# Norm parts at the seam between mixer 1 and block 1b moved; row minima of both mixers chained through a start value, masks added on VectorE

## The chip, the cores and the metric

The kernel runs on one core of a Trainium2 chip. The core has TensorE (PE; its weight loads are shown as PEld), VectorE (DVE), ScalarE (ACT), GpSimd (POOL) and the queue of SyncE (SP), which issues most DMAs. The metric is the device time of one execution in microseconds; lower is better.

## The reference

The model has two layers over 512 latent tokens and 256 context tokens, with 1024 channels. Each layer is a half SwiGLU block, an attention mixer and another half SwiGLU block; each of the three is modulated before and closed by a layer norm:

```python
def ffn_sublayer(h, shift, scale, gate, w_in, w_out, g, b):
    y = swiglu(modulate(h, shift, scale), w_in, w_out)
    return layer_norm(ALPHA * h + FFN_RES * gate * y, g, b)
```

Mixer 0 is neighbourhood attention: each query sees a window of 256 keys with a learned bias, and all 256 context keys. Mixer 1, the one at the centre of this case, works in blocks of 128 queries:

```python
valid = ((jnp.abs(pos_q[:, None] - pos_k[None, :]) <= WA_WINDOW)
         & (pos_k >= 0)[None, :] & (pos_k < S)[None, :])
s_win = jnp.where(valid, jnp.einsum('bqhgd,bkhd->bhgqk', qb, kb).astype(jnp.float32), NEG_INF)
s_ctx = jnp.einsum('bqhgd,bkhd->bhgqk', qb, kc).astype(jnp.float32)
s_sink = jnp.broadcast_to(sink, s_win.shape[:-1] + (1,))
p = jax.nn.softmax(jnp.concatenate([s_win, s_ctx, s_sink], axis=-1), axis=-1)
```

So a row of scores has up to 384 window keys, 256 context keys and one sink logit, and its maximum goes over all three. In layer 1 the context tokens need no output, so what follows mixer 1 handles the 512 latent tokens alone. The output is the latent stream after layer 1.

## The kernel before

**Layout.** Activations lie with channels on the 128 partitions and tokens along the row: eight tiles `z` for the stream. A matmul operand is split into a rounded part and a rest (`uh`, `ul` for activations, `wh`, `wl` for weights), and a full product is three matmuls (`mm3`, L160 to L167). Weights come by DMA on SP's queue into `wr`; ACT makes `wh` (L103) and POOL or DVE makes `wl` (L105).

**Order.** The stages are 0a, mixer 0, 0b, 1a, mixer 1, 1b. The program is written in an order of its own, and a scheduler that simulates the engines sets the final order of each engine's queue when the kernel is built. Two means steer it. `plan` (L147) hangs functions on named points, and `at` (L151) runs them when the program comes by, for example `wo7_3` (after the last attention block of head pair 7) or `pd1b_0_0_4` (after the fifth down product of 1b's first chunk). `behind` (L343) orders two instructions of one engine. `keep_back` holds an instruction behind which each following accumulation (`accumulate`, L499 to L502: z plus gate times product, on DVE) is ordered; `back` sets it.

**A layer norm** (`layer_norm`, L432, and `ln`) is a list of parts: sums over the eight `z` tiles (DVE and POOL, L352), the mean by a matmul with a matrix of 1/1024 (`pm`, L447), centring (L369) with squares on ACT (L456) and their sum, the variance by matmuls (`pv`, L472) with a reciprocal root by tiny DVE operations (`rstd`, L477 and L359 to L364), a spread of the root over the partitions by matmuls (`pr`, L400), then for each channel tile the normalisation (L485), the modulated `uf` (L319), `uh` (L321) and `ul` (L326), and last `kept`, which scales `z` for the residual (L340, POOL). In the lists `l4[0]` (tokens 0 to 255, after mixer 1) and `l4[1]` (tokens 256 to 511) the indices 0 to 6 are sums, mean, centring, variance, spread, normalisation with modulation, kept.

**The seam.** Mixer 1 handles the last two head pairs (6 and 7) in two halves of the tokens: attention for tokens 0 to 255, their output products (`pow`, `w3_0`), attention for tokens 256 to 511, their output products (`w3_1`, banks `c` and `s` in turn, four in all). Each half has eight output products of six matmuls. Block 1b then opens with tokens 0 to 255: two pairs of products `pa1b`, `pv1b` (24 matmuls each), eight down products `pd1b` (on the two banks of `s`), then the same for tokens 256 to 511. The first needs `l4[0]`, the second `l4[1]`.

**Attention of mixer 1** (`attn`, L1193). Each of 8 head pairs has four blocks, and each block two heads: 64 heads in all. The scores (negated, so that the row maximum is a minimum) go into a bank `s` by two matmuls for the window (L1213, L1214) and two for the context (L874, L875). The band mask is added by PE: an identity times a 128 x 128 mask in bf16, for the first and for the last 128 columns of the window (L1216, L1218), 96 such matmuls in all. Edge blocks (0 and 3) have 256 window columns beside 256 of the context in one bank, middle blocks (1 and 2) have 384, and their context scores go to a bank `c`. DVE takes the minimum (L1226, in middle blocks also L1222) and combines it with the sink (L1230, in middle blocks L1228). ACT computes the exponentials and their sums (L1238 to L1242), DVE the reciprocal, POOL scales (L917), PE transposes (L898), and PE multiplies by the values (L908).

**Attention of mixer 0** (`lat`, L993) does the like for 64 latent heads: a minimum over the context (L1019), a reduction that adds the bias and takes the minimum over the window (L1020), a tiny operation for the smaller of both (L1022), then the exponential (L1024).

**Buffers.** The tag `v` of phase `S` holds 256 columns a buffer: the value tiles of the mixers and the `uf` tiles of norms over 256 tokens, 9 buffers. `mk` is a working tile into which the mask is loaded; DVE casts it to bf16 (L1118).

Of the kernel before, what the change touches and what calls it, by code (L numbers as in the profile page):

```python
# [8 lines left out]
F32 = mybir.dt.float32  # L9
F32R = mybir.dt.float32r  # L10
BF16 = mybir.dt.bfloat16
I32 = mybir.dt.int32
AF = mybir.ActivationFunctionType
# [5 lines left out]
P = 128  # L19
# [10 lines left out]
BIG = 1e30  # L30
# [8 lines left out]
def hybrid_kernel(ctx: ExitStack, tc: tile.TileContext, h0, cc, crow, wmod, wmodt, bmod, lnp, wst,  # L39
# [13 lines left out]
    def t2(nm, tag="t2"):  # L53
        return tp.tile([P, 512], F32, tag=tag, name=nm, bufs={"t2": 6, "ln": 2, "sl": 2}[tag])
# [245 lines left out]
    def mod_out(nm, d, c0, c1, st, prm, rm=False, dd=None):  # L300
# [204 lines left out]
    def ffn(nm, groups, gt, mid, post, units=(), opened={}, head=None, apart=None):  # L505
# [312 lines left out]

        def back(x):
            keep_back[0] = x  # L820

# [68 lines left out]
    def vtile(nm):  # L890
        return ph["S"].tile([P, 256], F32, tag="v", name=nm, bufs=9)

# [26 lines left out]
    def small(tag, nm):  # L919
        return tp.tile([P, 2], F32, tag=tag, name=nm, bufs=4)  # L920
# [26 lines left out]
    def na_mixer(gt):  # L947
# [45 lines left out]
        def lat(qd, pr, st, oh, ol, cbs=range(4)):  # L993
# [15 lines left out]
            for cb in cbs:  # L1009
                pts = []  # L1010
                qc = slice(cb * P, (cb + 1) * P)
                for h in range(2):
# [7 lines left out]
                    nc.vector.tensor_tensor_reduce(out=ps[:, 0:256], in0=ps[:, 0:256], in1=nbs[h][:, (0, 1, 1, 2)[cb], :],  # L1020
                                                   scale=1.0, scalar=BIG, op0=ALU.add, op1=ALU.min, accum_out=m[:, 1:2])
                    nc.vector.tensor_tensor(out=m[:, 0:1], in0=m[:, 0:1], in1=m[:, 1:2], op=ALU.min)  # L1022
                    p = t2(f"p{nm}")
                    last_exp[0] = nc.scalar.activation(p[:], ps[:], AF.Exp, bias=m[:, 0:1], scale=-1.0, accum_out=l[:, 0:1])  # L1024
                    nc.vector.reciprocal(l[:, 0:1], l[:, 0:1])  # L1025
# [77 lines left out]

    mkb = cp.tile([P, 2, P], BF16, name="mkb")
    idb = cp.tile([P, P], BF16, name="idb")
    nc.vector.tensor_copy(idb[:], idn[:])

    def wa_mixer(gt):
# [3 lines left out]
        for i in range(2):  # L1112
            t = gp.tile([P, NL], F32, tag="gs", name=f"rc{i}", bufs=6)
            nc.sync.dma_start(t[:], ropec[:, i, :])
            rc.append(t)
        mk = t2("mk")
        nc.sync.dma_start(mk[:, 0:256], wmask[:])
        nc.vector.tensor_copy(mkb[:].rearrange("p a b -> p (a b)"), mk[:, 0:256])  # L1118

# [73 lines left out]
        def attn(s, q, oh, ol, bs=range(4), tags=("t", "mm")):  # L1193
# [5 lines left out]
            def sink(h):  # L1199
                return nsink[:, hd + 4 * h:hd + 4 * h + 1]  # L1200

            for b in bs:
# [5 lines left out]
                split = nw + NC > 512  # L1208
                mc, lc = (small("mc", f"mc{nm}"), small("lc", f"lc{nm}")) if split else (None, None)
                pw, pc = [], []  # L1210
                for h in range(2):
                    pb = bank("s", f"sw{nm}_{h}")
                    nc.tensor.matmul(pb[:, 0:nw], q[h][:, qc], k[h][:, k0:k1], start=True, stop=False)  # L1213
                    nc.tensor.matmul(pb[:, 0:nw], q[h][:, qc], k[2 + h][:, k0:k1], start=False, stop=False)  # L1214
                    if b > 0:
                        nc.tensor.matmul(pb[:, 0:P], idb[:], mkb[:, 0, :], start=False, stop=b == 3)  # L1216
                    if b < 3:
                        nc.tensor.matmul(pb[:, nw - P:nw], idb[:], mkb[:, 1, :], start=False, stop=True)  # L1218
                    pb2 = bank("c", f"sc{nm}_{h}")[:, 0:NC] if split else pb[:, nw:nw + NC]
                    scores(pb2, q[h], k[h], k[2 + h], qc, slice(NL, NT))  # L1220
                    if split:
                        nc.vector.tensor_reduce(out=mc[:, h:h + 1], in_=pb2, axis=AX.X, op=ALU.min)  # L1222
                        pc.append(pb2)
                        pb = pb[:, 0:nw]
                    mh = m[:, h:h + 1]
                    nc.vector.tensor_reduce(out=mh, in_=pb, axis=AX.X, op=ALU.min)  # L1226
                    if split:
                        x = nc.vector.scalar_tensor_tensor(out=mh, in0=mh, scalar=mc[:, h:h + 1], in1=sink(h), op0=ALU.min, op1=ALU.min)  # L1228
                    else:
                        x = nc.vector.tensor_tensor(out=mh, in0=mh, in1=sink(h), op=ALU.min)  # L1230
                    pw.append(pb)
# [168 lines left out]
    def whole(x, head):  # L1400
# [22 lines left out]
    plan(wa_4=l3[1][1:3], wa_7=l3[1][3:4], wq0_0=l3[1][4:6], wq0_1=l3[0][6:] + l3[1][6:])  # L1423
    plan(wo6_2=l4[0][:1], wo6_3=l4[0][1:2], wm7_3=l4[0][2:3], wo7_3=l4[0][3:4], pow3_1_256_2=l4[0][4:6],
         pow3_1_256_7=l4[1][:1])
    wa_mixer(gate(1, 5, 1.0))
    plan(pa1b_0_0_0=l4[0][6:], pv1b_0_0_0=l4[1][1:3], pd1b_0_0_3=l4[1][3:4], pd1b_0_0_7=l4[1][4:])
    ffn("1b", g1, lambda: gate(1, 8, 0.5), None, final, apart=True)
# [126 lines left out]
```

## Time and profile before

| What | Value |
|---|---|
| Median of three runs | 2750.59 us (2749.0 to 2759.77) |
| Profiled execution, own time | 2756.96 us |
| Its span, first to last instruction | 2755.2 us |
| Granted clock of TensorE, mean | 0.986 |
| Busy: PE, DVE, ACT, POOL | 2646.0, 1851.5, 1206.2, 1665.0 us |
| DMA | 311.92 MB, mean 113 GB/s |

Busy times are of one execution; the shares overlap, since the engines run side by side. In the slices of the profile each digit is a fortieth of the span (about 69 us) and gives the busy share in tenths. A PE that is busy is not necessarily at its peak: matmuls overlap in the pipeline, so their durations sum to more than their stretch of time. In a timeline the brackets show how long the engine stood idle before an instruction and what ended that.

### The profile page before, as it was taken

What the parts mean: (1) busy time and instruction counts of PE and PEld (TensorE: products, weight loads), DVE (VectorE), ACT (ScalarE), POOL (GpSimd) and SP (SyncE); (2) the same over time, 40 slices, a digit from 0 to 9 for tenths busy, and PEclk for the clock granted to TensorE, in tenths of its full rate; (3) what the DMA queues carried; (4) which work ended last, traced back from release to release, by engine and by line L of the source; (5) the groups of instructions that cost most, each with busy time, mean ns of one, the idle gap of its engine ahead of it and who ended that gap; (6) DMA issues with size and microseconds to landing.
All of it is one profiled execution on the core that took longest, in us unless ns stands there. A gap on an engine that the chain in (4) does not pass through costs nothing. (4 is left out here: it accounts for less than half of the span.)

```text
span 2755.2 us, 47890 instructions
## 1 busy us (share of the span) xinstructions
PE 2646.0 (96%) x16954; PEld 2415.7 (88%) x16954; DVE 1851.5 (67%) x4238; ACT 1206.2 (44%) x2505; POOL 1665.0 (60%) x1522
## 2 busy tenths in 40 slices
PE   8999999999999989999999999999998999899997
PEld 5799998887888889999998889999987777899997
DVE  4877777775555687656565766666577767677765
ACT  5244343366445344343432534343336655444442
POOL 4786766464433566867664668666645445567762
PEclk9999999999999999999999999999999999999998
DMA  9367565522221213444443225556632111245551
GB/s 330 93 176 200 141 167 148 149 78 66 58 58 49 72 47 93 117 126 128 120 135 106 75 77 146 141 143 179 192 118 64 32 32 45 64 104 127 135 144 56
DMA packets 295615, 311.92 MB, mean 113 GB/s; under 512 B 27856, under 2 KB 193872, under 8 KB 294352
## 3 DMA queue, kind: packets, MB, share of 16 engines
q1 hardware_dynamic: 278960, 279.36, 34.0%
q0 software_dynamic: 16128, 29.37, 6.4%
q8 instruction: 134, 2.20, 0.3%
q14 instruction: 105, 0.86, 0.1%
q10 hardware_dynamic: 288, 0.14, 0.0%
HBM read 300.92 MB, written 12.25 MB: 114 GB/s over the span
## 5 line engine op out<-in xcount | busy, mean ns | idle before, releaser
L105 POOL TENSOR_TENSOR wl<-wr,wh 128x512 fp32r<-128x512 f32 x200 | 261.1, 1322 | 155.9 <-ACT wh L103 78.1
L105 POOL TENSOR_TENSOR wl_s<-S,wh_s 128x512 fp32r<-128x512 f32 x240 | 317.8, 1360 | 45.4 <-ACT wh_s L103 44.9
L103 ACT CAST wh_s<-S 128x512 fp32r<-128x512 f32 x256 | 155.3, 620 | 415.6 <-POOL S L641 128.3
L641 POOL TENSOR_TENSOR S<-wr,wr 128x512 f32<-128x512 f32 x128 | 173.5, 1355 | 202.3 <-DMA wr<-in_wst_dram 188.3
L212 DVE CUSTOM_DVE_ANT_0 jk<-wt,cb 128x512 f32<-128x512 f32 x360 | 244.9, 680 | 22.8 <-DMA wt<-in_wmodt_dram 18.6
L105 POOL TENSOR_TENSOR wl_a<-wr,wh_a 128x512 fp32r<-128x512 f32 x144 | 189.1, 1361 | 15.6 <-ACT wh_a L103 12.7
L103 ACT CAST wh_a<-wr 128x512 fp32r<-128x512 f32 x192 | 118.7, 621 | 153.2 <-PE pd1b L166 20.2
L103 ACT CAST wh<-wr 128x512 fp32r<-128x512 f32 x200 | 121.0, 618 | 91.6 <-DMA wr<-in_wst_dram 17.5
L500 DVE SCALAR_TENSOR_TENSOR z<-pd0b,gt,z 128x256 f32<-128x256 f32 (+1 forms) x168 | 97.0, 595 | 43.0 <-PE pd0b L167 42.3
L500 DVE SCALAR_TENSOR_TENSOR z<-pd1a,gt,z 128x512 f32<-128x512 f32 (+1 forms) x150 | 88.7, 606 | 34.9 <-PE pd1a L167 27.5
L917 POOL TENSOR_SCALAR p<-p,l 128x512 f32<-128x512 f32 x64 | 44.4, 695 | 109.6 <-DVE l L1025 109.1
L500 DVE SCALAR_TENSOR_TENSOR z<-pd0a,gt,z 128x512 f32<-128x512 f32 (+1 forms) x160 | 93.4, 613 | 14.4 <-PE pd0a L167 14.1
L641 POOL TENSOR_TENSOR S<-wr,S 128x512 f32<-128x512 f32 x64 | 90.4, 1413 | 3.5
L641 POOL TENSOR_TENSOR S<-S,wr 128x512 f32<-128x512 f32 x64 | 90.3, 1411 | 3.1
L340 POOL TENSOR_SCALAR z<-z,ag_None,ab_None 128x256 f32<-128x256 f32 (+1 forms) x77 | 57.9, 755 | 51.2 <-DVE uh L325 33.6
L917 POOL TENSOR_SCALAR pw<-pw,l 128x512 f32<-128x512 f32 (+1 forms) x64 | 40.9, 640 | 76.2 <-DVE l L1252 31.6
L1024 ACT ACTIVATE p<-s,m 128x512 f32<-128x512 f32 x64 | 44.0, 688 | 81.5 <-DVE m L1022 76.7
L326 DVE TENSOR_TENSOR ul<-ufl,uh 128x256 fp32r<-128x256 f32 (+1 forms) x88 | 59.7, 685 | 6.9 <-ACT uh L321 5.4
L319 ACT ACTIVATE ufl<-z,bi_None,sc_None 128x256 f32<-128x256 f32 (+1 forms) x77 | 48.2, 638 | 26.1 <-DVE z L485 25.7
L500 DVE SCALAR_TENSOR_TENSOR z<-pd1b,gt,z 128x512 f32<-128x512 f32 (+1 forms) x91 | 53.3, 619 | 9.2 <-PE pd1b L167 6.6
L164 PE MATMUL vn<-wh,uh 128*128 128x256 f32 x192 | 54.9, 286 | 0.9 <-DVE nq L861 0.5
L166 PE MATMUL vn<-wl,uh 128*128 128x256 f32 x192 | 54.4, 283 | 0.0
(1488 smaller groups left out, 10636.2 us busy)
## 6 DMA issues: line engine op xcount, KB each, us to landing
wr<-in_wst_dram SPq DMA_DIRECT2D x456, 256.0 KB
wt<-in_wmodt_dram SPq DMA_DIRECT2D x206, 256.0 KB
wr_0b<-in_wst_dram SPq DMA_DIRECT2D x47, 256.0 KB
wr_1b<-in_wst_dram SPq DMA_DIRECT2D x47, 256.0 KB
wr_2b<-in_wst_dram SPq DMA_DIRECT2D x47, 256.0 KB
wr_3b<-in_wst_dram SPq DMA_DIRECT2D x47, 256.0 KB
wm<-in_wmod_dram SPq DMA_DIRECT2D x8, 1024.0 KB
zspare<-in_wmodt_dram SPq DMA_DIRECT2D x30, 256.0 KB
```

Of the source, the lines that this page charges most:

```text
L103: nc.scalar.copy(hi[:], src[:])
L105: x = eng.tensor_tensor(out=lo[:], in0=src[:], in1=hi[:].bitcast(F32), op=ALU.subtract)
L164: behind(nc.tensor.matmul(ps, a[0], b[0], start=first, stop=False), in_front[0])
L166: nc.tensor.matmul(ps, a[0], b[1], start=False, stop=False)
L212: x = nc.vector.tensor_tensor_reduce(out=junk[:], in0=w[:], in1=cb[st], scale=1.0, scalar=0.0, op0=ALU.mult, op1=ALU.add, accum_out=out[st])
L319: nc.scalar.activation(uv, zs, AF.Identity, scale=s1, bias=s2)
L326: return hi, nc.vector.tensor_tensor(out=lo, in0=uv, in1=uo.bitcast(F32), op=ALU.subtract)
L340: nc.gpsimd.tensor_scalar(out=zs, in0=zs, scalar1=prm[2][:, d:d + 1], scalar2=prm[3][:, d:d + 1], op0=ALU.mult, op1=ALU.add)
L500: last[0] = nc.vector.scalar_tensor_tensor(out=zt(d, c0, c1), in0=pd, scalar=gt[:, d, st:st + 1], in1=zt(d, c0, c1), op0=ALU.mult, op1=ALU ...
L641: nc.gpsimd.tensor_tensor(out=t[:], in0=a[:], in1=b[:], op=o)
L917: nc.gpsimd.tensor_scalar(out=p, in0=p, scalar1=r, scalar2=0.0, op0=ALU.mult, op1=ALU.add)
L1024: last_exp[0] = nc.scalar.activation(p[:], ps[:], AF.Exp, bias=m[:, 0:1], scale=-1.0, accum_out=l[:, 0:1])
```

## The change

Five things change together.

- In mixer 0 the minimum over the context is the start value of the reduction over the window, and the tiny operation L1022 is gone.
- In mixer 1 the mask matmuls and their bf16 tiles are gone. DVE adds the mask in a reduction over the window that starts from the sink, and a second reduction over the context, with a zero operand, starts from its result. Both also write their sums back to the bank. The separate minima and the operations with the sink are gone.
- The mask is held in a tile of its own, `mk3`: mask, zeros, mask (384 columns), loaded by two DMAs, with a POOL memset for the zeros. `nil`, the zero operand, is the middle part read twice. For it the tag `v` has 8 buffers from mixer 1 on.
- The accumulations of the first three output products of `w3_1` are ordered behind the root of `l4[0]`.
- Mean and centring of `l4[1]` go from the first `pv1b` product to the first `pa1b` product, the variance from the fourth down product to the end of the second `pv1b` product, spread, normalisation and kept from the eighth down product to the fourth.

```diff
-            uf = ph["S"].tile([P, 256], F32, tag="v", name=f"uf{nm}_{d}", bufs=9)
+            uf = ph["S"].tile([P, 256], F32, tag="v", name=f"uf{nm}_{d}", bufs=vbufs[0])
...
                     nc.vector.tensor_reduce(out=m[:, 0:1], in_=ps[:, 256:512], axis=AX.X, op=ALU.min)
                     nc.vector.tensor_tensor_reduce(out=ps[:, 0:256], in0=ps[:, 0:256], in1=nbs[h][:, (0, 1, 1, 2)[cb], :],
-                                                   scale=1.0, scalar=BIG, op0=ALU.add, op1=ALU.min, accum_out=m[:, 1:2])
-                    nc.vector.tensor_tensor(out=m[:, 0:1], in0=m[:, 0:1], in1=m[:, 1:2], op=ALU.min)
+                                                   scale=1.0, scalar=m[:, 0:1], op0=ALU.add, op1=ALU.min, accum_out=m[:, 1:2])
...
-        mk = t2("mk")
-        nc.sync.dma_start(mk[:, 0:256], wmask[:])
-        nc.vector.tensor_copy(mkb[:].rearrange("p a b -> p (a b)"), mk[:, 0:256])
+        vbufs[0] = 8
+        mk3 = ph["S"].tile([P, 3, P], F32, tag="mk", name="mk", bufs=1)
+        nc.gpsimd.memset(mk3[:, 1, :], 0.0)
+        for i in range(2):
+            nc.sync.dma_start(mk3[:, 2 * i, :], wmask[:, i, :])
+        mk = mk3[:].rearrange("p a b -> p (a b)")
+        nil = mk3[:, 1:2, :].broadcast_to([P, 2, P])
...
-                    nc.tensor.matmul(pb[:, 0:nw], q[h][:, qc], k[h][:, k0:k1], start=True, stop=False)
-                    nc.tensor.matmul(pb[:, 0:nw], q[h][:, qc], k[2 + h][:, k0:k1], start=False, stop=False)
-                    if b > 0:
-                        nc.tensor.matmul(pb[:, 0:P], idb[:], mkb[:, 0, :], start=False, stop=b == 3)
-                    if b < 3:
-                        nc.tensor.matmul(pb[:, nw - P:nw], idb[:], mkb[:, 1, :], start=False, stop=True)
+                    scores(pb[:, 0:nw], q[h], k[h], k[2 + h], qc, slice(k0, k1))
                     pb2 = bank("c", f"sc{nm}_{h}")[:, 0:NC] if split else pb[:, nw:nw + NC]
                     scores(pb2, q[h], k[h], k[2 + h], qc, slice(NL, NT))
+                    mh, mk0 = m[:, h:h + 1], 0 if b else P
+                    nc.vector.tensor_tensor_reduce(out=pb[:, 0:nw], in0=pb[:, 0:nw], in1=mk[:, mk0:mk0 + nw], scale=1.0,
+                                                   scalar=sink(h), op0=ALU.add, op1=ALU.min, accum_out=mc[:, h:h + 1])
+                    pb3 = pb2.rearrange("p (a b) -> p a b", a=2)
+                    x = nc.vector.tensor_tensor_reduce(out=pb3, in0=pb3, in1=nil, scale=1.0, scalar=mc[:, h:h + 1],
+                                                       op0=ALU.add, op1=ALU.min, accum_out=mh)
                     if split:
-                        nc.vector.tensor_reduce(out=mc[:, h:h + 1], in_=pb2, axis=AX.X, op=ALU.min)
                         pc.append(pb2)
                         pb = pb[:, 0:nw]
-                    mh = m[:, h:h + 1]
-                    nc.vector.tensor_reduce(out=mh, in_=pb, axis=AX.X, op=ALU.min)
-                    if split:
-                        x = nc.vector.scalar_tensor_tensor(out=mh, in0=mh, scalar=mc[:, h:h + 1], in1=sink(h), op0=ALU.min, op1=ALU.min)
-                    else:
-                        x = nc.vector.tensor_tensor(out=mh, in0=mh, in1=sink(h), op=ALU.min)
...
-    plan(wo6_2=l4[0][:1], wo6_3=l4[0][1:2], wm7_3=l4[0][2:3], wo7_3=l4[0][3:4], pow3_1_256_2=l4[0][4:6],
-         pow3_1_256_7=l4[1][:1])
+    plan(wo6_2=l4[0][:1], wo6_3=l4[0][1:2], wm7_3=l4[0][2:3], wo7_3=l4[0][3:4] + [lambda: back(last_rstd[0])],
+         pow3_1_256_2=[lambda: back(None)] + l4[0][4:6], pow3_1_256_7=l4[1][:1])
     wa_mixer(gate(1, 5, 1.0))
-    plan(pa1b_0_0_0=l4[0][6:], pv1b_0_0_0=l4[1][1:3], pd1b_0_0_3=l4[1][3:4], pd1b_0_0_7=l4[1][4:])
+    plan(pa1b_0_0_0=l4[0][6:] + l4[1][1:3], pv1b_0_1_0=l4[1][3:4], pd1b_0_0_3=l4[1][4:])
```

`back` moves unchanged from the SwiGLU function to the place where `keep_back` is made, so that both can call it.

More of the change, by code (lines that the diff above doesn't have):

```diff
@@ L10 @@
 F32R = mybir.dt.float32r
-BF16 = mybir.dt.bfloat16
 I32 = mybir.dt.int32
@@ L347, in behind, with back @@
                 mybir.DependencyClass.NoSync, mybir.DependencyReason.DATA), reason="order")
+    vbufs = [9]
     last_rstd, last_add, hold, keep_back = [None], [None], [None], [None]
+    def back(x):
+        keep_back[0] = x
     def add(eng, out, a, b):
@@ L817, in ffn @@
         added = last_add[0]
-        def back(x):
-            keep_back[0] = x
         if nb == 3:
@@ L890, in vtile @@
     def vtile(nm):
-        return ph["S"].tile([P, 256], F32, tag="v", name=nm, bufs=9)
+        return ph["S"].tile([P, 256], F32, tag="v", name=nm, bufs=vbufs[0])
     def transpose(nm, p, order, tags):
@@ L1020, in lat @@
                     nc.vector.tensor_tensor_reduce(out=ps[:, 0:256], in0=ps[:, 0:256], in1=nbs[h][:, (0, 1, 1, 2)[cb], :],
-                                                   scale=1.0, scalar=BIG, op0=ALU.add, op1=ALU.min, accum_out=m[:, 1:2])
-                    nc.vector.tensor_tensor(out=m[:, 0:1], in0=m[:, 0:1], in1=m[:, 1:2], op=ALU.min)
+                                                   scale=1.0, scalar=m[:, 0:1], op0=ALU.add, op1=ALU.min, accum_out=m[:, 1:2])
                     p = t2(f"p{nm}")
-                    last_exp[0] = nc.scalar.activation(p[:], ps[:], AF.Exp, bias=m[:, 0:1], scale=-1.0, accum_out=l[:, 0:1])
+                    last_exp[0] = nc.scalar.activation(p[:], ps[:], AF.Exp, bias=m[:, 1:2], scale=-1.0, accum_out=l[:, 0:1])
                     nc.vector.reciprocal(l[:, 0:1], l[:, 0:1])
@@ L1101, in na_mixer @@
         wo3(1)
-    mkb = cp.tile([P, 2, P], BF16, name="mkb")
-    idb = cp.tile([P, P], BF16, name="idb")
-    nc.vector.tensor_copy(idb[:], idn[:])
     def wa_mixer(gt):
@@ L1208, in attn @@
                 split = nw + NC > 512
-                mc, lc = (small("mc", f"mc{nm}"), small("lc", f"lc{nm}")) if split else (None, None)
+                mc, lc = small("mc", f"mc{nm}"), small("lc", f"lc{nm}") if split else None
                 pw, pc = [], []
```

## The prediction

> **What bounds the kernel now.** I read the page's busy times and slices first, then the waits of TensorE over the whole span, then the 10 us windows from the start of mixer 1 into block 1b, then the timelines of PE and DVE there.
>
> ```profile
> PE 2646.0 (96%) x16954; PEld 2415.7 (88%) x16954; DVE 1851.5 (67%) x4238; ACT 1206.2 (44%) x2505; POOL 1665.0 (60%) x1522
> PE   8999999999999989999999999999998999899997
> PE pa1b L164 <- ACT uh L321: 4.9, 2, 2.9
> ```
>
> PE is busy for 96% of 2755.2 us, so only two things shorten the run: fewer matmuls where PE is full, or shorter waits where it stands. The late dips of the slices are the first attention of mixer 1 and the seam from mixer 1 to 1b. Among the waits, that of 1b's first products (pa1b) for their input uh is the third: twice, 4.9 us in all.
>
> ```profile
> 2130.00:2140.00 10.00, 7.95 (x49) 6.27 (x50) 6.17 (x20) 7.49 (x24) 3.46 (x6) 0.60 0.00 0
> 2140.00:2150.00 10.00, 9.74 (x92) 7.93 (x91) 7.15 (x23) 6.59 (x21) 3.77 (x7) 1.00 0.01 2
> ...
> 2300.00:2310.00 10.00, 10.00 (x73) 7.83 (x74) 9.07 (x25) 6.52 (x22) 5.51 (x8) 1.00 0.20 54
> ...
> 2350.00:2360.00 10.00, 6.42 (x32) 6.21 (x32) 8.54 (x22) 7.33 (x17) 9.23 (x13) 0.66 0.36 102
> ```
>
> Columns: stretch, length, busy PE, PEld, DVE, ACT, POOL, then the granted clock. From 2140 to 2310 PE is full in most windows (14 of the 22 from 2130 to 2350 are at 9.6 or more, these two the first and the last): projections and output products fill the waits of attention. At 2350 it is busy for 6.42 of 10 us, at a clock of 0.66.
>
> **The seam, as it runs now.**
>
> ```profile
> 2348.15 0.28 PE L164 MATMUL pow<-woh,wh 128*128 128x256 f32 x1
> 2348.27 0.28 PE L166 MATMUL pow<-wol,wh 128*128 128x256 f32 x1
> ...
> 2350.66 0.71 PE L400 MATMUL prl<-idn,yl 128*128 128x128 f32 x4 [0.64 <-DVE yl L364]
> 2354.31 0.58 PE L164 MATMUL pa1b<-uh,wh 128*128 128x256 f32 x1 [2.94 <-ACT uh L321]
> ...
> 2359.60 0.42 PE L166 MATMUL pv1b<-ul,wh 128*128 128x256 f32 x1
> 2359.81 0.33 PE L167 MATMUL pv1b<-uh,wl 128*128 128x256 f32 x1
> ...
> 2374.41 0.50 PE L472 MATMUL pvl<-onesd,aql 128*128 128x1 f32 x4
> ...
> 2378.84 0.68 PE L400 MATMUL prl<-idn,yl 128*128 128x128 f32 x4 [0.74 <-DVE yl L364]
> 2381.45 0.39 PE L164 MATMUL pa1b<-uh,wh 128*128 128x256 f32 x1 [1.93 <-ACT uh L321]
> ```
>
> Columns: start, duration, instruction, in brackets PE's idle time before it. Norm l4_0 (tokens 0-255) runs variance, reciprocal root on DVE, spread (prl, 2350.66), normalisation, uh; PE waits 0.64 and 2.94 us. Then matmuls start 0.21 us apart (2359.60, 2359.81) where warm ones start 0.12 apart (2348.15, 2348.27), until 2359.97: 5.66 us at that rate hold work for 3.2, so the slow stretch costs 2.5 us more. Norm l4_1 (tokens 256-511) takes the same path: variance 2374.41, spread 2378.84, first product 2381.45, with waits of 0.74 and 1.93 us, not followed by a slow stretch.
>
> ```profile
> 2345.40 0.17 DVE L477 TENSOR_SCALAR pvl<-pvl 128x2 f32<-128x2 f32 x1 [1.72 <-PE pvl L472]
> ...
> 2345.80 0.15 DVE L359 TENSOR_SCALAR yl<-pvl 128x2 int32<-128x2 int32 x1
> 2345.99 0.17 DVE L362 TENSOR_TENSOR pvl<-pvl,yl 128x2 f32<-128x2 f32 x1
> ...
> 2347.80 0.87 DVE L500 SCALAR_TENSOR_TENSOR z<-pow,gt,z 128x256 f32<-128x256 f32 x2
> ...
> 2350.46 0.15 DVE L364 SCALAR_TENSOR_TENSOR yl<-pvl,yl 128x2 f32<-128x2 f32 x1
> ...
> 2373.12 0.42 DVE L352 TENSOR_TENSOR aql<-pml,sql 128x256 f32<-128x256 f32 x1
> ...
> 2378.55 0.15 DVE L364 SCALAR_TENSOR_TENSOR yl<-pvl,yl 128x2 f32<-128x2 f32 x1
> ```
>
> The root is 11 tiny DVE operations (L477, L359, then nine). Alone they follow each other 0.2 us apart (2345.80, 2345.99): 2.2 us. Now they take 5.2 us (2345.40 to 2350.61), since accumulations (L500, 0.43 each) lie between them.
>
> **Term A, l4_0.** The first three accumulations of the last output products go behind the root, so it should end near 2347.6, 3.0 us sooner. The price: the products use four banks, and the first frees about 1 us later, so PE stops before the fifth product; the spread (0.7 us) fits into that hole. Eight accumulations at 0.4 from 2347.6 let the last product end near 2350, as now. Spread to 2348.4, a normalisation (0.4, behind an accumulation or two), then on ACT 0.60 and 0.39:
>
> ```profile
> 2352.87 0.60 ACT L319 ACTIVATE ufl<-zspare,bi_None,sc_None 128x256 f32<-128x256 f32 x1 [2.31 <-DVE zspare L485]
> ...
> 2353.87 0.39 ACT L321 CAST uh<-ufl 128x256 fp32r<-128x256 f32 x1
> ```
>
> so the first uh comes near 2350.4, not 2354.3. That is 3.9 us plus the slow stretch's 2.5: 6.4. Queued behind the held accumulations on DVE are l4_1's sums and the normalisations; PE waits for both. I take -6.0; ends: -6.4, and +1.1 if PE only stops and nothing else moves.
>
> **Term B, l4_1.** Mean and centring go from the second product of 1b to the first; each is 24 matmuls at 0.12, 2.9 us, but PE runs them interleaved, so I take 1 us sooner; variance no longer waits from 2373.54 (aql's end) to 2374.41; variance and root together take 4.3 us (2374.41 to 2378.70), and about 0.6 + 2.2 once they are ordered before the accumulations of pd1b, 1.5 less. That is 3.4 us of chain, but no more PE time than the waits hold, 0.74 + 1.93 = 2.67. I take -2.0; ends: -2.7, and +1.0 if the last down products, with two banks, stop for root and normalisations, which now come before their accumulations.
>
> **Term C, mixer 1: 96 mask matmuls leave PE, the mask goes into DVE's row minimum.**
>
> ```profile
> 2297.71 0.28 PE L1213 MATMUL sw<-wk,wq 128*128 128x256 f32 x1
> ...
> 2298.30 0.39 PE L164 MATMUL pow<-woh,wh 128*128 128x512 f32 x1
> ...
> 2302.20 0.23 PE L1216 MATMUL sw<-mkb,idb 128*128 128x128 bf16 x1
> ...
> 2302.33 0.50 PE L898 MATMUL tpw<-idn,pw 128*128 128x128 f32 x3
> ```
>
> A matmul's duration overlaps its neighbours; what counts is the distance of starts. A head of an edge block (b = 0 or 3) takes 0.59 us for its five matmuls (2297.71 to 2298.30); four at 0.12 would take 0.48: 0.11 saved. A middle block's two masks take 0.13 (2302.20 to 2302.33). With 32 heads of each kind: 3.5 + 4.2 = 7.7 us of PE stream.
>
> ```profile
> L1226 DVE TENSOR_REDUCE m<-sw 128x1 f32<-128x512 f32 x32 | 21.6, 682 | 5.2 <-PE sw L875 5.1
> L1226 DVE TENSOR_REDUCE m<-sw 128x1 f32<-128x384 f32 x32 | 17.3, 548 | 1.6 <-PE sw L1218 1.2
> L1222 DVE TENSOR_REDUCE mc<-sc 128x1 f32<-128x256 f32 x32 | 13.2, 414 | 1.9 <-PE sc L875 1.9
> L1230 DVE TENSOR_TENSOR m<-m,nsink 128x1 f32<-128x1 f32 x32 | 9.9, 315 | 0.2
> L1228 DVE SCALAR_TENSOR_TENSOR m<-m,mc,nsink 128x1 f32<-128x1 f32 x32 | 9.3, 298 | 0.1
> ...
> L1020 DVE CUSTOM_DVE_ANT_0 s<-s,nb 128x256 f32<-128x256 f32 x64 | 27.2, 430 | 4.6 <-POOL nb L1004 3.5
> L1022 DVE TENSOR_TENSOR m<-m 128x1 f32<-128x1 f32 x64 | 17.7, 280 | 1.1
> L1020 DVE DVE_READ_ACCUMULATOR2_ANT m<- 128x1 f32 x64 | 8.9, 140 | 0.0
> ```
> ```profile
> L212 DVE CUSTOM_DVE_ANT_0 jk<-wt,cb 128x512 f32<-128x512 f32 x360 | 244.9, 680 | 22.8 <-DMA wt<-in_wmodt_dram 18.6
> ```
>
> DVE loses the first five groups, 71.3 us. It gains 64 reductions with the mask and 64 of the context, each of mixer 0's form (L1020: 0.43 for 256 columns, about 0.55 for 384, as the plain reduction) with 0.14 to read the result: 32 x 0.43 + 32 x 0.55 + 64 x 0.43 + 128 x 0.14 = 76.8 us. DVE's load is nearly the same, the wait for one head's minimum is not: edge 1.14 against 682 + 315 = 1.00 us, middle 1.25 against 548 + 298 = 0.85 where the context's minimum was taken early. All of it in the open would be 32 x 0.14 + 32 x 0.40 = 17.3 us, with ACT's exponential and the two s banks waiting. The form with a zero operand that repeats isn't in the trace: its nearest row is L1020, which I take; its far end is the same operation over 512 columns (L212, 0.68), as if each context column counted twice: 0.25 us more. In 14 of 22 windows PE is full, so 7.7 x 14 / 22 = 4.9 arrives; in the others the longer chain about cancels the rest. I take -5.0; ends: -7.7, and 17.3 - 7.7 = +9.6.
>
> **Term D, mixer 0.** L1022 goes, 64 x 0.28 = 17.7 us of DVE, 0.3 from each head's minimum. TensorE's waits in mixer 0 (560 to 990), the first and the last of 14 rows, of 19.9 us in all:
>
> ```profile
> PE o L908 <- DVE p L850: 3.8, 4, 2.4
> ...
> PE tp_c L898 <- POOL p_c L917: 0.2, 1, 0.2
> ```
>
> So it covers attention nearly everywhere. I take -1.5; ends: -5, a quarter of these waits, and +2, if the second reduction, which now needs the first's result, starts 0.03 us later in each of 64 heads.
>
> **Nothing** for the rest: two mask loads instead of one on SP's queue, a small POOL memset, two casts gone, one v buffer less; they lie beside the first products of mixer 1. [...] If the norm's uf tiles lacked a buffer, ACT would wait on DVE's ul, behind term A's chain.
>
> **Sum:** -6.0 - 2.0 - 5.0 - 1.5 = -14.5. The profiled execution took 2756.96 us (1.76 beside its span), so 2742.5 by its own time; that is 6.4 above the median of the three timed runs, 2750.59, from which the same sum gives **2736.1**. A measurement of this kernel can tell about 0.5% (13.8 us) from no change.
>
> **Rivals.**
> - *The mask's gain is eaten* by the longer chain of each head: C is 0, 2741.1. For it: at 2130 PE stands a fifth of the time with DVE busy for only 6.17, so the chain's length holds it, not DVE's load. Against: the full PE windows. 0.13.
> - *The seam stays*: the queues' order is set when the kernel is built, and spread and mean may still come after all products. A and B are 0: 2744.1. For it: now the spread stands behind all eight products. Against: it stood there because the root was late. 0.12.
> - *The slow clock stays* although the wait shrinks: +2.5, 2738.6. For it: at 2130 the clock is 0.60 with PE busy for 7.95 of 10. Against: 1.93 us at 2381 left it full. 0.09. [...]
> - *Slower: DVE becomes the bound of mixer 1.* The chained minimum lies open in all 64 heads and the repeated-zero form costs the far end: 17.3 + 64 x 0.25 = 33.3, masks worth nothing, seam -8.0, D -1.5: +23.8, 2774. It passes 0.5% from (13.8 + 9.5) / 64 = 0.36 us per head on. 0.11.
>
> **How the numbers follow.** The forecast case has 0.55, with its own range 2727 to 2743: 0.38 beyond 0.5%, 0.17 within. The eaten mask gives 0.02 and 0.11, the seam 0.02 and 0.10, the clock 0.03 and 0.06, the slower case 0.01 within and 0.10 beyond. Faster 0.45, same 0.45, slower 0.10. The range 2726 to 2752 reaches over the rivals up to the old time and leaves out the slower case and about 0.08 at the ends.
>
> **What would show it.** A: root under 3 us, spread before the last pow product, first pa1b under 1.5 us after it, clock near 1 in that window. B: second pa1b wait under 1 us. C: no bf16 matmuls, context minima at 0.43, no new PE waits on pw's exponential. D: PE waits in mixer 0 little changed. Wrong if the minima are longer than 0.5, or PE stands at pow for banks longer than the spread takes.

## The result, and the profile after

| | before | after |
|---|---|---|
| Median | 2755.44 us (2749.0 to 2759.77, 6 runs) | 2730.53 us (2723.34 to 2735.21, 6 runs) |
| Ratio after / before | | 0.9913, 95% interval 0.9896 to 0.993 |
| Profiled execution, own time | 2756.96 us | 2735.21 us |
| Its span | 2755.2 us | 2733.4 us |
| Granted clock of TensorE, mean | 0.986 | 0.988 |

The kernel became faster by 0.7 to 1.0%. The median lies inside the predicted range, 5.6 us below the forecast. But against the six runs of before that stand beside it the gain is 24.9 us (19 to 29 by the ratio's interval) where 14.5 were forecast, so terms were mis-sized; the parts below show that the one of mixer 0 was far too small. The profiled execution of after is the slowest of its six runs.

The busy times and the slices of TensorE, from the page of after (after's line numbers differ by a few: L163, L165, L166 are the three matmuls of `mm3`, L875 and L876 those of the scores, L503 the accumulation, L1232 the exponential of pw):

```profile
PE 2635.5 (96%) x16858; PEld 2406.7 (88%) x16858; DVE 1834.8 (67%) x4268; ACT 1206.9 (44%) x2505; POOL 1667.7 (61%) x1523
...
PE   7999999999999899999999999999998999899997
```

96 matmuls are gone (16,954 to 16,858), and 10.5 us of busy TensorE with them; VectorE has 16.7 us less, though it makes 30 instructions more. The late dips of the slices are where they were: the attention of mixer 1 and the seam have not filled up. The waits of TensorE over the whole span of after (engine, line, what it waited for: us in all, times, longest) say what keeps the attention from it:

```profile
PE sw L875 <- ACT pw L1232: 9.2, 12, 2.0
...
PE pa1b L163 <- ACT uh L320: 2.1, 2, 1.2
```

Block 1b's wait for its input fell from 4.9 to 2.1 us, as the seam's two terms wanted. A wait took its place that was small before: the scores of mixer 1 wait for a bank until ACT has made the exponential of an earlier head. In the kernel before the same wait stood at 2.4 us:

```profile
PE sw L1213 <- ACT pw L1238: 2.4, 2, 2.1
```

Stage by stage, each from one profiled execution; a stage goes from the first TensorE start of one tile to that of another (mixer 0: pq to pa0b; 0b: to pa1a; attention of mixer 1: first to last score sw; seam: from there to the last pa1b). Idle is the sum of the waits view in that stretch. The slow-clock loss is the length of each 4 us window times what its granted clock lacked to 1, summed up.

| | mixer 0, idle | 0b, idle | attention of mixer 1, busy, idle | seam, slow-clock loss |
|---|---|---|---|---|
| before | 422.2, 19.9 | 545.1, 7.8 | 206.4, 196.0, 9.8 | 86.6, 3.4 |
| after | 412.3, 14.7 | 541.9, 4.0 | 205.3, 188.4, 16.3 | 87.7, 8.5 |

So the time went in mixer 0 (9.9 us) and in 0b (3.2 us), where the forecast had put 1.5. Of the 9.9 us, 5.2 are shorter waits and 3.4 are slow clock (5.1 us lost before, 1.7 after), so this pair of profiles alone overstates what the change did there. In the attention of mixer 1 TensorE works 7.6 us less and stands 6.5 us more. Of the difference of the two spans, 21.8 us, another 4.1 lie ahead of mixer 0, where both kernels are the same (up to mixer 0, 565.7 and 561.6 us; 554.5 to 565.7 from one execution to another); the other stages differ by at most 2 us each.

The seam of after, first in windows of 10 us (busy PE, PEld, DVE, ACT, POOL, then the granted clock), then the timeline of TensorE and that of VectorE:

```profile
2309.30:2319.30 10.00, 7.54 (x53) 5.60 (x50) 6.39 (x29) 5.67 (x19) 5.34 (x8) 0.77 0.07 15
2319.30:2329.30 10.00, 7.85 (x65) 6.19 (x63) 6.64 (x18) 4.99 (x14) 3.37 (x4) 0.84 0.14 40
2329.30:2339.30 10.00, 9.42 (x46) 9.06 (x44) 6.05 (x22) 3.23 (x6) 4.47 (x5) 0.53 0.21 55
2339.30:2349.30 10.00, 8.38 (x66) 7.78 (x65) 8.25 (x18) 7.92 (x16) 8.55 (x11) 1.00 0.19 52
```
```profile
2333.72 0.58 PE L163 MATMUL pow<-woh,wh 128*128 128x256 f32 x1 [0.58 <-DVE z L503]
...
2335.16 1.05 PE L403 MATMUL prl<-idn,yl 128*128 128x128 f32 x4
...
2336.23 0.41 PE L165 MATMUL pow<-wol,wh 128*128 128x256 f32 x1
2336.44 0.41 PE L166 MATMUL pow<-woh,wl 128*128 128x256 f32 x1
...
2339.22 0.28 PE L166 MATMUL pow<-woh,wl 128*128 128x256 f32 x1
2340.39 0.39 PE L163 MATMUL pa1b<-uh,wh 128*128 128x256 f32 x1 [0.90 <-ACT uh L320]
...
2355.16 0.50 PE L163 MATMUL pd1b<-gh1b,wh 128*128 128x256 f32 x2 [1.34 <-ACT gh1b L532]
...
2364.71 0.39 PE L163 MATMUL pa1b<-uh,wh 128*128 128x256 f32 x1 [1.22 <-ACT uh L320]
```
```profile
2330.41 0.17 DVE L480 TENSOR_SCALAR pvl<-pvl 128x2 f32<-128x2 f32 x1 [2.55 <-PE pvl L475]
...
2333.18 0.48 DVE L503 SCALAR_TENSOR_TENSOR z<-pow,gt,z 128x256 f32<-128x256 f32 x1 [1.21 <-PE pow L166]
...
2334.16 0.16 DVE L367 SCALAR_TENSOR_TENSOR yl<-pvl,yl 128x2 f32<-128x2 f32 x1
```

The spread (prl) now lies among the last output products, and the first product of 1b waits 0.90 us instead of 2.94. The price is there too: a stop of 0.58 us for a bank. But the output products themselves run 0.21 us apart (2336.23, 2336.44), at a granted clock of 0.53: the slow stretch, which lay behind the wait before, lies ahead of it now.

### The profile page after: what moved, and what is told of

Its sections match the earlier page's. It is cut to its first block, busy times and chain, and to the rows that moved or that the text cites. A ratio compares the mean times of both kernels' runs of the same rounds, so it can differ in the third digit from the quotient of the medians.

```text
span 2733.4 us, 47740 instructions
## 1 busy us (share of the span) xinstructions
PE 2635.5 (96%) x16858; PEld 2406.7 (88%) x16858; DVE 1834.8 (67%) x4268; ACT 1206.9 (44%) x2505; POOL 1667.7 (61%) x1523
## 4 chain that ended last, share of the span: by engine, by line
PE 56%; DVE 6%; ACT 2%; issue 1%; DMA 1%; POOL 0%; DVEq 0%; SPq 0%; ACTq 0%; POOLq 0%
PE pd0b L165 2%; PE pd0b L163 2%; PE pd0b L166 2%; PE pd1a L163 2%; PE pd1a L165 2%; PE pd1a L166 2%; PE pd1b L163 1%; PE wo L909 1%; PE pd1b L165 1%; PE pd1b L166 1%; DVE z L503 1%; PE tpw L899 1%; PE sw L875 0%; PE wq L163 0%; PE wq L166 0%
## 5 line engine op out<-in xcount | busy, mean ns | idle before, releaser
L104 POOL TENSOR_TENSOR wl_a<-wr,wh_a 128x512 fp32r<-128x512 f32 x144 | 189.0, 1359 | 18.9 <-ACT wh_a L102 16.7
L503 DVE SCALAR_TENSOR_TENSOR z<-pd0b,gt,z 128x256 f32<-128x256 f32 (+1 forms) x168 | 96.7, 594 | 38.2 <-PE pd0b L166 37.9
L503 DVE SCALAR_TENSOR_TENSOR z<-pd1a,gt,z 128x512 f32<-128x512 f32 (+1 forms) x150 | 88.6, 605 | 37.4 <-PE pd1a L166 36.6
L503 DVE SCALAR_TENSOR_TENSOR z<-pd0a,gt,z 128x512 f32<-128x512 f32 (+1 forms) x160 | 93.6, 611 | 15.7 <-PE pd0a L166 15.4
L503 DVE SCALAR_TENSOR_TENSOR z<-pd1b,gt,z 128x512 f32<-128x512 f32 (+1 forms) x91 | 53.2, 618 | 9.7 <-PE pd1b L166 8.2
L318 ACT ACTIVATE ufl<-z,bi_None,sc_None 128x256 f32<-128x256 f32 (+1 forms) x77 | 48.1, 637 | 25.2 <-DVE z L488 24.9
L104 DVE TENSOR_TENSOR wl_a<-wr,wh_a 128x512 fp32r<-128x512 f32 x48 | 51.6, 1086 | 6.3 <-ACT wh_a L102 6.3
L163 PE MATMUL vn<-wh,uh 128*128 128x256 f32 x192 | 54.7, 285 | 1.1 <-DVE nq L862 0.6
```

The costliest lines, as they stand in the source:

```text
L104: x = eng.tensor_tensor(out=lo[:], in0=src[:], in1=hi[:].bitcast(F32), op=ALU.subtract)
L163: behind(nc.tensor.matmul(ps, a[0], b[0], start=first, stop=False), in_front[0])
L318: nc.scalar.activation(uv, zs, AF.Identity, scale=s1, bias=s2)
L503: last[0] = nc.vector.scalar_tensor_tensor(out=zt(d, c0, c1), in0=pd, scalar=gt[:, d, st:st + 1], in1=zt(d, c0, c1), op0=ALU.mult, op1=ALU ...
```

## The experiments

All kernels were timed in 5 rounds beside the kernel before, in three groups of four, each group on one chip; the median of before was 2752.04, 2752.11 and 2749.36 us in them. Stage lengths are of one profiled execution each, measured as above. "Moved" counts the instructions of TensorE's queue within a stage that stand in another order as built than in the kernel before (the fewest whose removal leaves the same order).

**Each part alone.** The chain of mixer 0 (term D) alone:

```diff
-                                                   scale=1.0, scalar=BIG, op0=ALU.add, op1=ALU.min, accum_out=m[:, 1:2])
-                    nc.vector.tensor_tensor(out=m[:, 0:1], in0=m[:, 0:1], in1=m[:, 1:2], op=ALU.min)
+                                                   scale=1.0, scalar=m[:, 0:1], op0=ALU.add, op1=ALU.min, accum_out=m[:, 1:2])
...
-                    last_exp[0] = nc.scalar.activation(p[:], ps[:], AF.Exp, bias=m[:, 0:1], scale=-1.0, accum_out=l[:, 0:1])
+                    last_exp[0] = nc.scalar.activation(p[:], ps[:], AF.Exp, bias=m[:, 1:2], scale=-1.0, accum_out=l[:, 0:1])
```

> The kernel before with the chained minimum in mixer 0 alone (64 tiny operations on DVE gone). Theory from the two traces: mixer 0 got 9.9 us shorter, so this part alone gives 8 to 12 us (ratio 0.9955 to 0.997), with TensorE's waits in mixer 0 near 15 instead of 20 us and fewer slow-clock stretches there. Rival, the prediction's own term D: 1.5 us (ratio 0.9995), and mixer 0's difference in the traces is a chance of the clock.

Measured: 2735.59 us, ratio 0.9949 (0.993 to 0.9969). Mixer 0 took 413.2 us (422.2 before), with 14.3 us of waits, and 0b 542.3. This one part brings some 14 us, the largest gain of the change's parts.

The move of the mask in mixer 1 alone (term C: the hunks of `wa_mixer` with `mk3`, and nothing else of the change):

> The kernel before with the masks of mixer 1 moved from PE to DVE alone. Theory from the traces: PE's busy time in mixer 1 falls by 7 to 8 us but its waits for ACT's exponential grow by 6 to 7, so the gain is 0 to 2 us (ratio 0.999 to 1.000). Rival, term C of the prediction: 5 us (ratio 0.998).

Measured: 2750.02 us, 0.9995 (0.998 to 1.0011). The attention took 205.4 us (206.4 before), busy 188.7, idle 16.1: of the 7.3 us that the mask matmuls freed, TensorE stood 6.3.

Terms A and B together (the last two `plan` hunks and `back`):

> The kernel before with the moved norm parts alone (held accumulations and earlier parts of the second norm). Prediction, terms A and B: 8 us (ratio 0.997), with no slow clock at 1b's first products. Rival: the held accumulations stop PE at its four banks and the slow clock only moves forward into the output products, so 2 to 4 us (ratio about 0.999).

Measured: 2745.39 us, 0.9978 (0.9965 to 0.999), about 6 us. Each of them alone:

```diff
+         wo7_3=l4[0][3:4] + [lambda: back(last_rstd[0])],
+         pow3_1_256_2=[lambda: back(None)] + l4[0][4:6], pow3_1_256_7=l4[1][:1])
```

> The kernel before with the accumulations held behind the root alone (term A). As predicted: -6 us, ratio 0.9978 (2746). By the runs so far (term B alone and both together gave 0.9978 each) A is worth nothing by itself: ratio 0.9990 to 1.0010 (2749 to 2755), the first wait of pa1b for uh stays between 1.5 and 3 us or the slow clock only changes its place.

Measured (A alone): 2746.74 us, 0.9993 (0.9979 to 1.0007), no difference that can be told. In its profile the first wait for uh is 0.99 us, and from the last score to the first product of 1b 18.3 us pass where 20.4 passed before:

```profile
2340.07 0.39 PE L164 MATMUL pa1b<-uh,wh 128*128 128x256 f32 x1 [0.99 <-ACT uh L321]
```

```diff
-    plan(pa1b_0_0_0=l4[0][6:], pv1b_0_0_0=l4[1][1:3], pd1b_0_0_3=l4[1][3:4], pd1b_0_0_7=l4[1][4:])
+    plan(pa1b_0_0_0=l4[0][6:] + l4[1][1:3], pv1b_0_1_0=l4[1][3:4], pd1b_0_0_3=l4[1][4:])
```

> The kernel before with the parts of the second norm alone issued earlier; accumulations are not held. Term B of the prediction: 2 us (ratio 0.9993), the second wait of pa1b under 1 us. Rival: it carries most of the 6 us that the moved parts gave together (ratio about 0.998) and the held accumulations give nothing, since PE stops for banks and its clock falls.

Measured (B alone): 2746.23 us, 0.9978 (0.9965 to 0.9992), as much as both together. The profiled execution of B alone, 2751.95 us, lost 10.2 us to the slow clock in the seam, so its gain is read from the ratio. From the first to the last product pa1b it took 64.3 us (66.2 before); the second wait for uh is what it was:

```profile
2374.98 0.39 PE L164 MATMUL pa1b<-uh,wh 128*128 128x256 f32 x1 [1.93 <-ACT uh L321]
```

The change without the mask (chain and seam together, masks on TensorE):

> The changed kernel with the masks of mixer 1 back on PE: chained minimum in mixer 0 and the moved norm parts. If the mask's move is worth nothing, this is as fast as the changed kernel (ratio 0.991 to 0.993 to the kernel before); if it is worth the 5 us of term C, this is 5 us slower than the changed kernel (ratio 0.993 to 0.995); if it costs, this beats it (under 0.990).

Measured: 2734.38 us, 0.9937 (0.9915 to 0.9959). The product of the three parts is 0.9949 x 0.9995 x 0.9978 = 0.9922, and the whole has 0.9913 (0.9896 to 0.993): the parts add up within the intervals. For the mask this ratio says less than it seems: by the expectation 0.9937 speaks for a mask worth 5 us, against what the mask alone showed, and its interval overlaps that of after. The stage speaks for nothing gained: the attention of mixer 1 took 205.4 us here, with the masks on TensorE, and 205.3 in the kernel after.

**Why the chain in mixer 0 gained nine times its forecast.** Three kernels take apart what the chain changes: the tiny operation's time, its stalls, the dependency, and the order of the queues. First the tiny operation with one operand passed as a pointer to a scalar, then twice in a row, then the chain with the tiny operation kept behind it:

```diff
-                    nc.vector.tensor_tensor(out=m[:, 0:1], in0=m[:, 0:1], in1=m[:, 1:2], op=ALU.min)
+                    nc.vector.tensor_scalar(out=m[:, 0:1], in0=m[:, 0:1], scalar1=m[:, 1:2], scalar2=None, op0=ALU.min)
```

> The kernel before, with mixer 0's tiny operation kept but fed one of its two operands as a per-partition scalar. In the trace of before the tiny operation has a median of 160 ns and a mean of 280 ns, since some of the 64 last over 1 us. If those stalls are what the chained minimum removed, this form should show a mean near 160 ns and give about half or more of the 14 us of the chained minimum (ratio 0.995 to 0.998). If the number of dependent operations before the exponential counts, or the order of the queues, it gives less than 3 us (0.999 to 1.000).

Measured: 2750.38 us, 0.9991 (0.9978 to 1.0005); mixer 0 420.5. The tile view of the line in the kernel before and in this one (count: shortest, median and longest in ns) shows that the stalls are gone all the same:

```profile
L1022 DVE TENSOR_TENSOR m<-m x64: 146/160/1329, 622.2 to 970.3; 128x1 f32<-128x1 f32 x64
```
```profile
L1022 DVE TENSOR_SCALAR m<-m x64: 194/214/216, 612.7 to 958.3; 128x1 f32<-128x1 f32 x64
```

With two columns as operands the operation takes 160 ns at the median but 1329 at worst; with a pointer none takes over 216. The trace of before shows what ran beside the long ones. In each of the 18 that took over 250 ns a GpSimd instruction was running when it began, and it ended within 20 ns of that one's end; the longest:

```profile
927.92 1.53 POOL L1004 TENSOR_TENSOR nb<-nmask_sb,nb 128x768 f32<-128x768 f32 x1
...
928.13 1.33 DVE L1022 TENSOR_TENSOR m<-m 128x1 f32<-128x1 f32 x1
```

Eight others of the 64 also began while a GpSimd instruction ran and took 150 to 238 ns; why the 18 were held up and these were not is not shown. With the pointer the stalls went, and no gain that can be told came.

```diff
+                    nc.vector.tensor_tensor(out=m[:, 0:1], in0=m[:, 0:1], in1=m[:, 1:2], op=ALU.min)
                     nc.vector.tensor_tensor(out=m[:, 0:1], in0=m[:, 0:1], in1=m[:, 1:2], op=ALU.min)
```

> The kernel before with mixer 0's tiny operation done twice, 64 more of 0.28 us on DVE in front of the exponentials. If each such operation costs on the path, mixer 0 gets longer by about what the chained minimum took away: 6 to 12 us (ratio 1.002 to 1.0045), with TensorE's waits there near 25 us. If the gain was a lucky order of the queues, no change or either sign (0.9985 to 1.0015).

Measured: 2747.89 us, 0.9986 (0.997 to 1.0001); mixer 0 416.8, although each head's minimum takes 0.33 us longer and VectorE has 20.6 us more to do (groups of this kernel in mixer 0: busy us, mean ns, idle before):

```profile
L1023 DVE TENSOR_TENSOR m<-m 128x1 f32<-128x1 f32 x64 | 20.6, 329 | 1.2
L1022 DVE TENSOR_TENSOR m<-m 128x1 f32<-128x1 f32 x64 | 17.2, 273 | 1.0
```

```diff
+                                                   scale=1.0, scalar=m[:, 0:1], op0=ALU.add, op1=ALU.min, accum_out=m[:, 1:2])
+                    nc.vector.tensor_tensor(out=m[:, 1:2], in0=m[:, 0:1], in1=m[:, 1:2], op=ALU.min)
```

> The kernel before with the chained start value in mixer 0, but with the tiny operation kept behind it (it takes the smaller of two values of which the second is already the smaller): the dependency is that of the chained kernels, VectorE's work is that of before. As built, TensorE's queue in mixer 0 stands as in the kernel before (77 of some 2,720 instructions in other places, against 418 for the chain alone). If the order of the queues brings the 14 us: mixer 0 takes 420 to 422 us, block 0b 545, ratio 0.998 to 1.001 (2747 to 2755). If the dependency brings them: mixer 0 412 to 414, 0b 542, ratio 0.993 to 0.996 (2733 to 2741). If the removed operation on the path brings them: as the first, since it is still there; the double tiny operation, which was no slower, speaks against that already.

Measured: 2750.45 us, 0.9994 (0.998 to 1.0009); mixer 0 420.7. The dependency alone brings nothing that can be told, in all or in mixer 0. Block 0b took 542.5 us, though, where the expectation had 545 if the order decides. Its queue is not the old one in this kernel (126 of some 3,180 moved, 186 with the chain alone), and no slow clock fell on it, where before's 0b lost 1.7 us; so the 3 us of 0b are not put down to the order of mixer 0. Laid side by side, the length of mixer 0 goes by the order of its queue:

| TensorE's queue in mixer 0, of some 2,720 | kernels | mixer 0, us | less its slow-clock loss |
|---|---|---|---|
| as before (0 to 77 moved) | before, mask alone (both orders, see below), A + B, tiny with pointer, A, B, chain with tiny kept | 420.5 to 422.5 | 417.0 to 419.0 |
| 438 moved | tiny twice | 416.8 | 413.4 |
| 418 moved | chain alone, chain and seam, after, two more below | 412.3 to 413.3 | 409.8 to 410.7 |

Some 1.4 us between the first row and the last are only the border: with the chain 12 matmuls of mixer 0, at 0.12 us each, stand behind the first product of 0b. They do so in the two kernels with 77 moved too, and those stay in the first row.

What the new order does is seen in the waits of TensorE in mixer 0, in the kernel before, with the chain alone, and with chain and tiny operation:

```profile
PE pq L164 <- DVE nq L861: 2.8, 2, 1.4
PE pk L164 <- DVE nl L869: 2.6, 4, 0.8
```
```profile
PE o L908 <- DVE p L850: 3.9, 2, 2.7
PE tp L898 <- POOL p L917: 2.4, 3, 1.9
...
PE pk L164 <- DVE nl L869: 1.1, 2, 0.6
```
```profile
PE o L908 <- DVE p L850: 5.7, 6, 2.4
PE pq L164 <- DVE nq L861: 2.9, 2, 1.4
...
PE pk L164 <- DVE nl L869: 2.6, 4, 0.8
```

Projections (pq, pk) that waited for VectorE's nq and nl do so no more, or half as long, with the chain alone; with chain and tiny operation they wait as in the kernel before. The price of the chained reduction itself is small: a start value by pointer makes it 489 ns where the constant made it 430.

```profile
L1020 DVE CUSTOM_DVE_ANT_0 s<-s,nb,m 128x256 f32<-128x256 f32 x64 | 31.1, 489 | 9.5 <-POOL nb L1004 8.3
```

**Why the mask brought nothing.** In mixer 1 the order of the two reductions of a head is swapped, the context first from the sink, the window with the mask from its result; first in the kernel after, then with the move of the mask alone:

```diff
-                    nc.vector.tensor_tensor_reduce(out=pb[:, 0:nw], in0=pb[:, 0:nw], in1=mk[:, mk0:mk0 + nw], scale=1.0,
-                                                   scalar=sink(h), op0=ALU.add, op1=ALU.min, accum_out=mc[:, h:h + 1])
                     pb3 = pb2.rearrange("p (a b) -> p a b", a=2)
-                    x = nc.vector.tensor_tensor_reduce(out=pb3, in0=pb3, in1=nil, scale=1.0, scalar=mc[:, h:h + 1],
-                                                       op0=ALU.add, op1=ALU.min, accum_out=mh)
+                    nc.vector.tensor_tensor_reduce(out=pb3, in0=pb3, in1=nil, scale=1.0, scalar=sink(h),
+                                                   op0=ALU.add, op1=ALU.min, accum_out=mc[:, h:h + 1])
+                    x = nc.vector.tensor_tensor_reduce(out=pb[:, 0:nw], in0=pb[:, 0:nw], in1=mk[:, mk0:mk0 + nw], scale=1.0,
+                                                       scalar=mc[:, h:h + 1], op0=ALU.add, op1=ALU.min, accum_out=mh)
```

> The changed kernel with the two reductions of mixer 1 in the other order: the context first, from the sink, then the window with the mask from its result. If the longer chain behind the last scores holds the exponential and so PE (16 us of waits in the attention stretch against 9.8 before), the context's reduction can be done early in the middle blocks: waits fall by 3 to 6 us and the ratio to the kernel before is 0.989 to 0.990. If DVE's load and not the chain's order is what holds PE, it stays at the changed kernel's 0.991 to 0.992.

Measured: 2726.01 us, 0.9903 (0.9886 to 0.9921); attention 197.5 us, idle 10.9.

> The kernel before with the move of the mask alone, as in the earlier run of it (0.9995), but with the context's reduction first and the window's with the mask last. If the place in the chain decided that the mask brought nothing: attention of mixer 1 falls from 205 to 198 us, TensorE's waits in it from 16 to 11, ratio 0.996 to 0.998 (2741 to 2747). If the better time of the earlier kernel with this order was chance or needed the chain of mixer 0: attention 205, ratio 0.999 to 1.001 (2749 to 2755).

Measured: 2735.79 us, 0.995 (0.9934 to 0.9967), where the other order had 0.9995 (0.998 to 1.0011); attention 197.3 us, idle 11.8. The intervals don't touch. The wait that had eaten the gain, in the attention with the window first and with the context first:

```profile
PE sw L875 <- ACT pw L1233: 9.5, 12, 2.2
```
```profile
PE sw L875 <- ACT pw L1233: 5.0, 7, 2.6
```

So neither VectorE's load nor the price of the reductions held the gain back; these are the same in both kernels, 616 to 618 ns over 384 columns and 484 to 489 over 256. What decided is the swap. It also gives some 140 of 1,100 instructions of TensorE's queue in this attention another place as built, and TensorE's busy time there falls from 188.7 to 185.3 us for the same matmuls, so what follows directly from the chain and what from the order of the queue is not told apart here. The attention shows 9.1 us of the 13.7 that the ratio gives; the interval goes from 9 to 18 us.

Last, the best kernel so far without term A:

> The kernel after with the context's reduction first in mixer 1 and without term A. If A is worth nothing: the same as the earlier kernel with that order, ratio 0.989 to 0.992 (2722 to 2730). If A still brings its 3 to 6 us once the mask leaves TensorE: ratio 0.992 to 0.994 (2730 to 2736).

Measured: 2724.66 us, 0.9904 (0.9887 to 0.9921), the same as with A. These two kernels have the lowest medians of the study, some 5 us below after, but their ratios' intervals overlap with after's.

## Why the prediction was right or wrong

| Term | forecast | alone, from its ratio |
|---|---|---|
| A, l4_0 | -6.0 | -1.9 (-5.8 to +1.9) |
| B, l4_1 | -2.0 | -6.1 (-9.6 to -2.2) |
| A + B | -8.0 | -6.1 (-9.6 to -2.8) |
| C, mask | -5.0 | -1.4 (-5.5 to +3.0) |
| D, mixer 0 | -1.5 | -14.0 (-19.3 to -8.5) |

- **D was the term that failed.** The step "So it covers attention nearly everywhere" took the order of mixer 0's queues as given and bounded the gain by a quarter of the waits, 5 us. The order was not given: an edit of one tiny operation made the scheduler lay out mixer 0 anew, 418 instructions of TensorE stand elsewhere, waits fell from 19.9 to 14.3 us, and block 0b, whose queue changed too, took 3 us less. With the order of before, the chain brings nothing that can be told (0.9994), and neither does an operation without its stalls (0.9991). A third order, which the tiny operation done twice brought about, makes mixer 0 5.4 us shorter although the work is more. Of the four candidates only the order goes with the time of mixer 0; that it is the cause of all of it is inferred, since the new order could not be run with the tiny operation unchanged, and a share of the last 4 us, from 416.8 to 413, may belong to the shorter minimum. The expectation "PE waits in mixer 0 little changed" was wrong.
- **C went the way of the rival "the mask's gain is eaten".** The first half held to the tenth: 7.7 us of TensorE stream forecast, 7.6 us of busy time gone. The second half, "in 14 of 22 windows PE is full, so 4.9 arrives", failed: 6.5 of the 7.6 us came back as waits, and the attention got 1.1 us shorter. The ratio alone would leave the 5 us possible (-5.5 to +3.0); the stage lengths speak against them. The predicted sign of failure was there, waits for the exponential of pw. Its reason was only half right: the rival had the longer chain, 17.3 us if all lay open, yet with the context first the chain has the same two reductions and TensorE's waits fall from 16.1 to 11.8 us. The reductions were dearer than taken (485 to 489 against 430 ns over 256 columns, 616 to 618 against 550 over 384); the repeated zero operand costs nothing over the plain one (486 against 485), so the far end of 0.25 us is out, and the slower rival with it.

```profile
L1217 DVE CUSTOM_DVE_ANT_0 sw<-sw,mk,nsink 128x384 f32<-128x384 f32 x32 | 19.5, 618 | 2.1 <-PE sw L876 1.7
...
L1220 DVE CUSTOM_DVE_ANT_1 sc<-sc,mk,mc 128x256 f32<-128x256 f32 x32 | 15.4, 486 | 0.7
L1217 DVE CUSTOM_DVE_ANT_0 sw<-sw,mk,nsink 128x256 f32<-128x256 f32 x32 | 15.4, 485 | 8.4 <-PE sw L876 8.2
...
L1220 DVE DVE_READ_ACCUMULATOR2_ANT m<- 128x1 f32 x63 | 8.8, 140 | 0.0
```

- **A was right in its mechanism and mis-sized.** The spread moved ahead of the last output products, and the first pa1b waits 0.90 to 0.99 us in all five kernels with A. In three of them the root took 2.9 us (context first, A alone, A + B), under the 3 that were to show it; in after's profile it took 3.9 (2330.41 to 2334.32), since one accumulation (2333.18) among its operations waited 1.21 us for TensorE, whose granted clock was 0.53 from 2329.3 to 2339.3. But the first product of 1b came 2.1 us sooner in A's own profile, not 3.9: TensorE stopped 0.58 us for a bank, and 0.99 us of wait stayed. The 2.5 us of the slow stretch are not A's to win: the seam lost 1.7 us with A alone and 8.5 in after, 3.4 before. "Clock near 1 in that window" was wrong for after's profile: it was 0.53.
- **B went the way that was forecast, by more, and only in part as told.** The spread (0.74 before) no longer waits in any profile with B. The second wait of pa1b was to fall "under 1". In the two kernels with B and without A it stays 1.93 us. With both terms it is gone in the profiles of chain and seam and of context first, 1.22 in after's and 1.93 in that of A + B. The 1.9 us by which B's profile is shorter from the first to the last pa1b fit the forecast; where the rest of the 6.1 (2.2 to 9.6) comes from, no profile shows. The context-first kernel has one wait of pa1b for uh left, the first:

```profile
PE pa1b L163 <- ACT uh L320: 1.0, 1, 1.0
```

The earlier norm parts have their price: a down product waits 1.34 us for gh1b (2355.16 above), and the timeline of ACT shows what stands ahead of gh1b, squares of the norm (L459):

```profile
2354.13 0.39 ACT L459 ACTIVATE pml<-z 128x256 f32<-128x256 f32 x1 [0.29 <-DVE z L372]
2354.45 0.40 ACT L459 ACTIVATE sql<-z 128x256 f32<-128x256 f32 x1
2354.76 0.35 ACT L532 CAST gh1b<-pv1b 128x256 fp32r<-128x256 f32 x1
```

- **The slow clock stayed**, as a rival had it, only elsewhere. The clock records in the traces of before and after hold two values, 1 and 0.5. Within each of these two executions the slow stretches begin whole multiples of 3.41 us apart (to within 0.14 us), and each but the last lasts 3.41 us or a multiple of it: in mixer 0 and 0b of before they begin at 919.5, 953.6 and 1011.6 and last 3.41, 6.83 and 3.41. In before's seam the clock fell at 2353.1, only 1.7 us into the wait of 2.94. The wait of 1.93 us ahead of the second pa1b was no sure sign of a full clock either: in before the clock stayed at 1 after it, and in the profile of B alone, with the same wait, a slow stretch began 0.7 us after its end. So the length of a wait does not settle whether the clock falls; what does is not shown. Executions of the same kernel, with the same queues, differ in their mean clock: after's six runs go from 2723.34 us at 0.992 to 2735.21 at 0.988; 0.004 of 2730 us is 10.9 us, about the whole difference of 11.9. Over the 23 to 29 runs of before in each group, time and mean clock are correlated at -0.59 to -0.71, so the clock is a large part of the spread and not all of it. In the seam the loss was 8.5 us in after's profile and none in that of the kernel with the context first, whose seam differs from after's in nothing that the change put there.

That the total still fell into the range is luck: D was 12.5 us too small, the others together 5.5 us too large (13.0 against 1.4 + 6.1), and the range reached 10 us below the forecast. The start helped: the three runs of before had a median of 2750.59 us, the six beside the result 2755.44. A range laid around the latter would have begun at 2731, just above what was measured.

## What to carry to other kernels

Where a scheduler lays out the queues when the kernel is built, an edit is not only its own cost: compare the order of the queues as built before and after, and price the waits that the new order removes or makes, before counting the operation itself. Work taken off a full engine is worth only what does not turn into waits there (here 6.5 of 7.6 us did); try both orders of a chained reduction, and read the waits of the engine behind it rather than the load of the engine that does it. And a stage whose slow clock differs from one profile to another, as in this seam (8.5 us lost in after's, none with the context first), has to be judged from the ratio of many runs, not from one profile.

## What was not expected of the hardware

- In mixer 0 the reduction that starts from a value in a tile took 489 ns over 256 columns (the chain alone), the one that starts from a constant 430 (before): 0.06 us more, and reading the result was another 0.14.
- The tiny operation over one column with two columns as inputs had a median of 160 ns and a longest of 1329 in before, and each of the 18 over 250 ns ended within 20 ns of a GpSimd instruction that ran when it began; with one column and a pointer median and longest were 214 and 216.
- In the profiles of before and after the slow stretches began multiples of 3.41 us apart. In before the clock fell 1.7 us into the wait of 2.94, and not at the wait of 1.93; in the profile of B alone it fell 0.7 us after the end of the wait of 1.93.
- Between executions of the same kernel the time goes in large part with the mean granted clock, 0.988 to 0.992 for 12 us in after. Block 0a, the same in all kernels, took 565.7 us in before's profile, with 23.1 us of waits and 8.5 us lost to the slow clock, and 555.3 in that of the kernel after with the context first, with 13.9 us of waits and no slow clock.
